# One transformer layer on one core: the last SiLUs through the exponential, sums and gate operands at other steps

## The chip, the cores and the metric

One core of one Trainium2 chip runs the whole kernel. The metric is the device time of one execution, in microseconds (us), as the median of several runs. The engines are PE (TensorE, matrix products), ACT (ScalarE), DVE (VectorE), POOL (GpSimd) and SP (SyncE, here the queue that issues nearly all transfers). Each engine executes its own instructions strictly in the order in which they stand.

## The reference

One layer over 2048 tokens of width 1024 (the rotary turning, the gates' running maxima and the norms' details are left out):

```
xn   = rms_norm(h) ; proj = xn @ w_in
q, k = split(silu(dwconv3(proj[q, k columns])))        # 1024 channels, width 3
y_a  = sigmoid(o) * rms_norm(mlstm_fwd(q, k, v) + mlstm_bwd(q, k, v))   # chunks of 128
y_b  = softmax((qn @ kn.T + qr @ kr.T) * scale) @ v     # 4 heads
h   += concat(y_a, y_b) @ w_out
u    = dwconv3(rms_norm(h) @ w_up) ; h += (silu(gate) * val) @ w_down
gate = sigmoid(rms_norm(h) @ w_ple_gate)
h   += gate * rms_norm(p @ w_ple_proj)
out  = rms_norm(h)
```

All inputs and outputs are float32. SiLU of x is x * sigmoid(x), which equals x / (1 + exp(-x)).

## The kernel before, in words

**Products.** A float32 operand is split into a high and a low half that PE can take at full rate (`split`, lines 116 to 124: ACT casts the high half, DVE subtracts to get the low one; `split_g` does it with a gain), and a product is three matrix products of halves. The large products (`w_out`, `w_up`, `w_down`, `w_ple_gate`) go in blocks by a scheme of seven products for a 2x2 block matrix; its operands B11, T1, T2, B21, T3, T4, B22 are four blocks of the weight and four sums of blocks, which were worked out before by `sum4` (line 1184) and stored.

**Order.** The stages are: `in_proj` (to about 521 us), attention with the mLSTM worked in between, the output product, the up product, the down product, and the gate with the end. Python generators are advanced in fixed places of the program text: `tail` (line 454) is what `in_proj` leaves over for the attention loop, one step at each `pump` of `attend`; `other` are the mLSTM's steps. A scheduler then sets the order on each engine from the program's order and its dependencies. Buffers go by tags: a tile of a tag waits for the last reader of the tile before it.

**The tail.** `in_proj` works through eight groups of 128 channels (j = 0 to 7) in four quarters of the tokens (c). `taps(j, c)` makes the three taps of the convolution on a 128x512 tile `ct` (one ACT, two DVE instructions); `silu(j, c, t)` applies SiLU on ACT and stores the tile to `qk_d`, from which the mLSTM loads. For j = 7 the quarters c = 2, 1, 0 are left to `tail`. Softmax of the attention needs the exponential on ACT (L934, `pe<-bk,nm`, four in each tile); its negated maximum `nm` comes from four maxima `mx<-bk` on DVE (L916), its output is transposed by PE (`tb`), split into `pt` (ACT cast and DVE L123) and multiplied (`ppv`). The mLSTM's state products are `mb<-v,kk` (L764) and its state update `cb` (L768).

**`Out.beside`** (line 1698) is called at seven places `at` of each pair of token blocks of the output product (pairs i = -8 to -1). Among other things it advances `sums(0)`: four times (k = 0 to 3) a load of four blocks of a weight with its norm's factor (`tsum`), in the next step five DVE instructions (L1196 to L1203) and four stores to `t_d`.

**`Gate.beside`** (line 1923) does the same for the gate's pairs q, from q = -9 on, alongside the down product. `proj` makes the 32 products of p with `w_ple_proj` (`fs<-pw,ph`, six matrix products each, for 16 token blocks st and two halves f); their weights lie in the places x13 and x5, the gain `gpost` in x3. `load_op` (line 1268) splits the operands of one name, `op_begin` starts a block's list of operand loads (`opr`), `op_fill` keeps up to four of them loaded ahead. For the gate (blk 6) `op_begin` was called behind the seventh place of q = -2 by the loop of `stream`. In the pair q = -1 the weights of the first gate pair are made: PE transposes of the hidden tiles (`fs<-ident,ha`), a copy to `gwr`, a split to `fw<-gwr`, and from `gwr` sums of it for the block scheme.

Of the kernel before, what the change touches and what calls it, by code (L numbers as in the profile page):

```python
# [11 lines left out]
F32R = mybir.dt.float32r  # L12
BF16 = mybir.dt.bfloat16
AF = mybir.ActivationFunctionType
ALU = mybir.AluOpType
# [4 lines left out]
P = 128  # L20
# [15 lines left out]
SB = 512  # L36
# [6 lines left out]
def pause(n):  # L43

    for _ in range(n):
        yield
# [6 lines left out]
def _rot(kind, idx):  # L53
    idx = list(idx)
    i = 0
    while True:
        yield f"{kind}{idx[i % len(idx)]}"
        i += 1


class Block:
# [114 lines left out]
    def in_proj(self):  # L176
        nc, d = self.nc, self.d
# [146 lines left out]
        for st in range(NT):  # L324
# [3 lines left out]
            t = self.at(next(trot), [P, 512], name="vo")  # L328
# [7 lines left out]
        for st in range(NT):  # L336
            ps = nat(st, ws, 512)
            t = self.at(next(trot), [P, 512], name="vo")
# [62 lines left out]
        def conv(j, c):  # L401
            silu(j, c, taps(j, c))

        def taps(j, c):
            t = self.at(next(trot), [P, 512], name="ct")
            uu, o = us[j, c // 2], (c % 2) * 512
            nc.scalar.activation(t, uu[:, o:o + 512], AF.Identity, bias=cwt[:, 3, j:j + 1], scale=cwt[:, 0, j:j + 1])
            for tap in (1, 2):
                nc.vector.scalar_tensor_tensor(t, uu[:, o + tap:o + tap + 512], cwt[:, tap, j:j + 1], t,
                                               op0=ALU.mult, op1=ALU.add)  # L410
            return t

        def silu(j, c, t):
            nc.scalar.activation(t, t, AF.Silu)
            nc.sync.dma_start(self.qk_d[4 * c:4 * c + 4, :, j, :].rearrange("c p t -> p c t"),
                              t.rearrange("p (c t) -> p c t", t=P))

# [36 lines left out]
        def tail(other):  # L454

            for i in range(2):
                self.split_kv(vals, (2 + i,))
                yield
            yield from itertools.islice(other, 7)
            ts = []  # L460
            for c in (2, 1, 0):
                ts.append(taps(7, c))
                yield
            yield from pause(3)
            for c, t in zip((2, 1, 0), ts):
                silu(7, c, t)
            yield from pause(2)
            yield from other

        return tail  # L470
# [616 lines left out]
    def split_ops(self, names):  # L1087

        items = [(n, k) for n in names for k in range(4)]
        raws = []  # L1090
        for j in range(-4, len(items)):
            if j + 4 < len(items):
                n, k = items[j + 4]
                raws.append(self.at(next(self.orot), [P, SB], name="opr"))
                self.nc.sync.dma_start(raws[-1], self.op_source(0, n, k))
            if j < 0:
                continue
            if j == 0:
                yield
            n, k = items[j]  # L1100
            if k == 0:
                self.xop[n] = self.op_places(0, n)
            self.split(raws[j], *self.xop[n][k])
            yield

# [112 lines left out]
        kt = k + i // 2 * 4  # L1218
        return self.d["w_ple_gate"][0, kt * P:(kt + 1) * P, i % 2 * SB:i % 2 * SB + SB]

    def op_places(self, blk, n):

        kk = self.BLOCKS[blk][2]
        out = []
        self.units = getattr(self, "units", {})
        for k in range(kk):
            x = self.OPX3[n][k] if kk == 3 else (self.OPXG if blk == 6 else self.OPX)[n][k // 2]
            key = blk, x
            if key not in self.units:
                self.units[key] = [self.at(f"x{x}", [P, 2, 2, SB], F32R, "op"), 0]  # L1230
            t, e = self.units[key]
            self.units[key][1] += 1
            out.append((t[:, e, 0], t[:, e, 1]))
        return out

    def op_source(self, blk, n, k):
        i = int(n[1]) - 1 if n[0] == "T" else 2 * (int(n[1]) - 1) + int(n[2]) - 1
# [10 lines left out]
    def op_begin(self, blk):  # L1248

        self.items = [(blk, n, k) for n in ("B11", "T1", "T2", "B21", "T3", "T4", "B22") for k in range(self.BLOCKS[blk][2])]  # L1250
        self.loaded, self.tag = [], None
        self.op_fill()

    def op_fill(self):

        while self.items and len(self.loaded) < 4:
            blk, n, k = self.items[0]
            if not k and (blk, n) in self.RAWS and self.tag is None:
                self.orot = _rot("t", self.RAWS[blk, n])
            self.tag = self.tag or next(self.orot)  # L1260
            if self.tag in [t for *_, t in self.loaded]:
                return
            raw = self.at(self.tag, [P, SB], name="opr")
            self.nc.sync.dma_start(raw, self.op_source(blk, n, k))
            self.loaded.append((self.items.pop(0), raw, self.tag))
            self.tag = None

    def load_op(self, blk, n):

        ops = self.xop[n] = self.op_places(blk, n)  # L1270
        for k, (hi, lo) in enumerate(ops):
            item, raw, _ = self.loaded.pop(0)
            assert item == (blk, n, k)
            gain = {1: self.g2, 2: self.g2, 6: self.g3}.get(blk)
            if gain is not None and n[0] == "B":
                kt = k + (int(n[1]) - 1) * 4
                self.split_g(raw, gain[0][:, kt:kt + 1], hi, lo)
            else:
                self.split(raw, hi, lo)
            self.op_fill()  # L1280

    def up_load(self, i):

# [116 lines left out]
    def stream(self, out):  # L1400

        nc = self.nc
# [3 lines left out]
        NUP, blocks = self.NUP, self.BLOCKS  # L1406
# [90 lines left out]
        prev, n = None, blocks[-1][0] + blocks[-1][1]  # L1497
# [7 lines left out]
        NG = NUP + 24  # L1505
        for i in range(blocks[0][0], n):
            blk = max(q for q, bl in enumerate(blocks) if bl[0] <= i)
            j = i - blocks[blk][0]
# [102 lines left out]
                    next(steps[i])  # L1611
            load(then, "T3")
            side(7)
            if any(bl[0] + bl[1] - 2 == i for bl in blocks[:-1]):
                self.op_begin(blk + 1)
            prev = s

# [20 lines left out]
class Out:  # L1638
# [59 lines left out]
    def beside(self, s, at, bank):  # L1698
        b, i = self.b, s.i
        if i > 1:  # L1700
            return

        c = 2 * i + 15 if at == 5 else 2 * i + 14
        if at in (5, 7) and 0 <= c < NT:
            self.scaled(c)
        c, f = {7: (2 * i + 15, 0), 1: (2 * i + 13, 1), 2: (2 * i + 12, 0), 3: (2 * i + 12, 1)}.get(at, (-1, 0))
        if 0 <= c < NT:
            self.turn(c, f, bank)
        if (i, at) == (-8, 1):
            self.load(-7)  # L1710
        if i < 0 and at == 5:
            self.load_x(i, 1)
            (self.load if i < -2 else b.up_load)(i + 2)
        if i < -1 and at == 6:
            self.load_x(i + 1, 0)
        if i < 0 and at == 7:
            self.tiles = self.next
        if (i, at) == (-7, 7):
            b.load_taps()
        if (i, at) == (-5, 4):  # L1720
            b.ffn_taps(bank)
        if (i, at) == (-3, 4):
            self.sums = b.sums(0)
        if (i, at) in ((-3, 4), (-3, 6), (-3, 7), (-2, 1), (-2, 2), (-2, 3), (-2, 4), (-2, 6)):
            next(self.sums)


class Gate:
# [194 lines left out]
    def beside(self, s, at, bank):  # L1923

        b, i = self.b, s.i
        q = i - self.first
        if (q, at) == (-9, 3):
            self.load_weights()
        if (q, at) == (-8, 7):
            self.split_weights()  # L1930
        if (q, at) == (-7, 2):
            self.gpost = b.row_bcast(b.at("x3", [P, D], name="gpf"), self.d["ple_post_g"][0], D)
            self.ph[0] = self.prep_p(0)
        if -7 <= q < -1 and at < 7:
            n = (q + 7) * 6 + at - 5
            if 0 <= n < 2 * NT:
                self.proj(*divmod(n, 2), bank)
        if q == -2 and at == 7:
            self.load_tile(0)
            self.load_tile(1)  # L1940

        if -1 <= q < 7 and at in (1, 2, 4, 5):
            e, f = divmod(at - 1 if at < 3 else at - 2, 2)
            self.turn(i + 1, e, f, bank)
            if f and q + e > -1 and 2 * q + e + 4 < NT:
                self.load_tile(2 * q + e + 4)
        if q == 1 and at == 1:
            self.gfin = [b.row_bcast(b.at(f"t{f}", [P, SB], name="gfin"), self.d["final_g"][f * SB:f * SB + SB], SB)
                         for f in range(2)]
        if q == -1 and at == 7:  # L1950
            self.load_tile(2)
            self.load_pj()
            self.load_pj()
        if q >= 0 and at in (2, 4):
            s.h.append(self.load_h(2 * q + at // 2 - 1))
        if q == 1 and at == 1:
            self.gfin = [b.row_bcast(b.at(f"t{f}", [P, SB], name="gfin"), self.d["final_g"][f * SB:f * SB + SB], SB)
                         for f in range(2)]
# [48 lines left out]
```

## Time and profile before

| | |
|---|---|
| runs of the kernel | 2918.75, 2919.41, 2920.72 us; median 2919.41 |
| profiled execution | 2923.7 us |
| its span on the core | 2921.9 us |
| mean granted clock of TensorE | 0.996 |
| busy: PE, DVE, ACT, POOL | 98%, 70%, 52%, 5% |

Starts in the rows are microseconds from the span's start. A bracket at a row's end is idle time of the engine ahead of the instruction, and what ended it. TensorE's granted clock (PEclk) is 1.00 at its upper level, 2.4 GHz, and half of that at its lower one; a window's value is the mean over it.

### The profile page before, as it was taken

To read this page: it belongs to the slowest core of one execution; us is meant where nothing else is said; L and a number is where in the kernel's file an instruction comes from. 1 tells how busy PE (TensorE), PEld (TensorE's weight loads), DVE (VectorE), ACT (ScalarE), POOL (GpSimd) and SP (SyncE) were. 2 spreads that over 40 slices of the span, in tenths; PEclk is the share of its full clock that TensorE was granted. 3 is DMA by queue.
4 is the path that set the end of the run, shared out by engine and by line. 5 is a ranking of instruction groups with operands and counts; after the bars stand their busy time and mean duration, and the time that the engine had idled before them with its cause. 6 is when DMAs were issued, how large, how long until landed. Compare 5 with 4: busy or idle time off the path is not lost.

```text
span 2921.9 us, 41161 instructions
## 1 busy us (share of the span) xinstructions
PE 2866.5 (98%) x14654; PEld 2424.6 (83%) x14654; DVE 2035.5 (70%) x3765; ACT 1528.3 (52%) x2984; POOL 155.1 (5%) x295
## 2 busy tenths in 40 slices
PE   8999999999999999999899999999999999999998
PEld 7888888888888889888688888888888788888787
DVE  7521555777777777766677887867777867576777
ACT  7311544656666666755655555755555423254655
POOL 3100000000000010001100000000000000001111
PEclk9999999999999999999999999999999999999999
DMA  6612545653333333467955553757776757486764
GB/s 186 132 58 80 156 117 168 205 162 114 112 108 103 96 106 113 129 215 245 307 177 173 176 190 135 230 163 229 238 238 206 247 170 266 158 265 205 268 215 162
DMA packets 406014, 513.20 MB, mean 176 GB/s; under 512 B 33824, under 2 KB 267312, under 8 KB 405808
## 3 DMA queue, kind: packets, MB, share of 16 engines
q1 hardware_dynamic: 405808, 510.57, 55.1%
q8 instruction: 115, 1.88, 0.3%
q14 instruction: 91, 0.75, 0.1%
HBM read 328.35 MB, written 182.12 MB: 175 GB/s over the span
## 4 chain that ended last, share of the span: by engine, by line
PE 83%; DMA 6%; DVE 5%; ACT 3%; issue 2%; POOL 1%; SPq 0%; ACTq 0%; POOLq 0%; DVEq 0%
PE fy L1419 19%; PE fz L1419 13%; PE bk L133 13%; PE fx L1419 13%; PE ppv L133 5%; PE tb L974 3%; PE bk L911 2%; PE bk L915 2%; PE bk L913 2%; PE bk L912 2%; PE bk L914 2%; PE fs L133 1%; PE gb L133 1%; PE mb L849 1%; DMA h_d<-xt 1%
## 5 line engine op out<-in xcount | busy, mean ns | idle before, releaser
L1419 PE MATMUL fz<-op,fw 128*128 128x512 f32 x1968 | 479.2, 391 | 8.1 <-ACT fw L120 4.9
L1419 PE MATMUL fx<-op,fw 128*128 128x512 f32 x1968 | 479.6, 391 | 0.9 <-ACT op L128 0.7
L1419 PE MATMUL fy<-op,fw 128*128 128x512 f32 x1968 | 475.6, 390 | 1.7 <-ACT ug L1561 1.5
L1419 PEld LDWEIGHTS fz<-op,fw 128*128 128x128 f32 x1968 | 368.3, 188 | 85.7 <-ACT fw L120 6.1
L1419 PEld LDWEIGHTS fy<-op,fw 128*128 128x128 f32 x1968 | 368.7, 188 | 79.4 <-ACT ug L1561 1.9
L1419 PEld LDWEIGHTS fx<-op,fw 128*128 128x128 f32 x1968 | 369.0, 188 | 78.1 <-ACT op L128 1.9
L1419 PE MATMUL fy<-op,fwd 128*128 128x512 f32 (+1 forms) x984 | 238.0, 390 | 3.3 <-DVE uv L1404 1.7
L120 ACT CAST pt<-tb 128x512 fp32r<-128x512 f32 x256 | 147.2, 586 | 167.9 <-PE tb L974 167.2
L133 PE MATMUL bk<-wsp,xh 128*128 128x512 f32 (+1 forms) x768 | 234.4, 386 | 0.0
L916 DVE TENSOR_REDUCE mx<-bk 128x1 f32<-128x512 f32 x256 | 175.0, 685 | 64.4 <-PE bk L915 60.2
L1419 PEld LDWEIGHTS fy<-op,fwd 128*128 128x128 f32 x984 | 182.7, 188 | 42.1 <-DVE uv L1404 2.8
L133 PE MATMUL ppv<-pt,kv 128*128 128x256 f32 x1536 | 206.5, 288 | 1.8 <-ACT pt L120 1.5
L123 DVE TENSOR_TENSOR pt<-tb,pt 128x512 fp32r<-128x512 f32 x256 | 174.4, 685 | 29.8 <-ACT pt L120 27.7
L934 ACT ACTIVATE pe<-bk,nm 128x512 f32<-128x512 f32 x256 | 174.5, 694 | 35.9 <-DVE nm L928 32.4
L133 PEld LDWEIGHTS ppv<-pt,kv 128*128 128x128 f32 x1536 | 190.2, 192 | 2.5 <-ACT pt L120 1.8
L133 PEld LDWEIGHTS bk<-wsp,xh 128*128 128x128 f32 x768 | 145.4, 189 | 25.1
L133 PE MATMUL bk<-wsp,xl 128*128 128x512 f32 (+1 forms) x384 | 150.8, 393 | 8.4 <-DVE xl L123 8.4
L133 PE MATMUL bk<-xh,wqk 128*128 128x512 f32 x480 | 157.4, 393 | 0.0
L974 PE MATMUL tb<-ident,pe 128*128 128x128 f32 x1024 | 151.4, 274 | 4.8 <-DVE pt L123 4.1
L974 PEld LDWEIGHTS tb<-ident,pe 128*128 128x128 f32 x1024 | 122.0, 141 | 24.3 <-DVE pt L123 6.3
L120 ACT CAST fw<-hraw 128x1024 fp32r<-128x1024 f32 (+1 forms) x72 | 70.2, 981 | 119.0 <-PE fx L1419 61.2
L123 DVE TENSOR_TENSOR fw<-fwr,fw 128x1024 fp32r<-128x1024 f32 x88 | 107.5, 1221 | 24.1 <-ACT fw L120 24.1
(360 smaller groups left out, 4925.5 us busy)
## 6 DMA issues: line engine op xcount, KB each, us to landing
fwr<-in_w_up SPq DMA_DIRECT2D x66, 512.0 KB, 4.8
fh<-h_d SPq DMA_DIRECT2D x48, 512.0 KB, 4.6
h_d<-fh SPq DMA_DIRECT2D x48, 512.0 KB, 3.6
s_d<-fwr SPq DMA_DIRECT2D x44, 512.0 KB, 2.8
fws<-s_d SPq DMA_DIRECT2D x44, 512.0 KB, 3.7
rw<-row_d SPq DMA_DIRECT2D x32, 512.0 KB, 5.5
tw_d<-tsum SPq DMA_DIRECT2D x60, 256.0 KB, 5.4
opr<-tw_d SPq DMA_DIRECT2D x60, 256.0 KB, 4.9
```

The lines of the kernel that those rows point to most:

```text
L120: nc.scalar.copy(hi, src)
L123: (sub or nc.vector).tensor_tensor(lo, src, _f(hi), op=ALU.subtract)
L133: mm = lambda *a, **k: self.nc.tensor.matmul(*a, **k, skip_group_check=more)
L911: mm(ps, ql, kh[:, ks], start=True, stop=False)
L912: mm(ps, qr, self.krl[:, ks], start=False, stop=False)
L913: mm(ps, qh, kl[:, ks], start=False, stop=False)
L914: mm(ps, qr, self.kr2[:, ks], start=False, stop=False)
L915: mm(ps, qh, kh[:, ks], start=False, stop=True)
L916: nc.vector.tensor_reduce(s.mx[:, kb:kb + 1], ps, axis=AX.X, op=ALU.max)
L934: nc.scalar.activation(s.pe[:, kb % 2], s.banks[kb], AF.Exp, bias=s.nm, scale=ASCALE, accum_out=s.rs[:, kb:kb + 1])
L974: nc.tensor.transpose(t[:, j, :], s.p[kb][:, j * P:(j + 1) * P], self.ident)
L1419: nc.tensor.matmul(out, a[:, k * P:(k + 1) * P], parts[lo][:, cols], start=first, stop=lo == 1 and k == last, skip_group_check=more)
```

## The change

Three edits. First, the tail's three SiLUs become exp(-x) on ACT, into a tile `ce` of tag t6, and on DVE a clamp with the added one, a reciprocal and a product; each is spread over more steps of the generator. Second, the steps of `sums(0)` in `Out.beside` are taken at other places, so that two or three places lie between a load and its sums. Third, the gate's projection products are made two places sooner, and `op_begin` for the gate is called at the fifth place of q = -2; at places 6 and 7 the operands k = 2 and 3 of B11, T2 and T3 are split. `op_place` now takes one k at a time. The rest of the diff is the same code in another form.

```diff
         def silu(j, c, t):
             nc.scalar.activation(t, t, AF.Silu)
+            store_qk(j, c, t)
+
+        def store_qk(j, c, t):
             nc.sync.dma_start(self.qk_d[4 * c:4 * c + 4, :, j, :].rearrange("c p t -> p c t"),
...
             for c in (2, 1, 0):
                 ts.append(taps(7, c))
                 yield
-            yield from pause(3)
+
             for c, t in zip((2, 1, 0), ts):
-                silu(7, c, t)
-            yield from pause(2)
+                e = self.at("t6", [P, 512], name="ce")
+                nc.scalar.activation(e, t, AF.Exp, scale=-1.0)
+                yield
+                nc.vector.tensor_scalar(e, e, 1.0e38, 1.0, op0=ALU.min, op1=ALU.add)
+                nc.vector.reciprocal(e, e)
+                yield
+                nc.vector.tensor_tensor(t, t, e, op=ALU.mult)
+                store_qk(7, c, t)
             yield from other
...
     def op_begin(self, blk):
 
         self.items = [(blk, n, k) for n in ("B11", "T1", "T2", "B21", "T3", "T4", "B22") for k in range(self.BLOCKS[blk][2])]
+        self.soon, self.early = (blk == 6) * [(blk, n, k) for n in ("B11", "T2", "T3") for k in (2, 3)], {}
+        self.items = self.soon + [item for item in self.items if item not in self.soon]
         self.loaded, self.tag = [], None
         self.op_fill()
...
     def load_op(self, blk, n):
 
-        ops = self.xop[n] = self.op_places(blk, n)
-        for k, (hi, lo) in enumerate(ops):
-            item, raw, _ = self.loaded.pop(0)
-            assert item == (blk, n, k)
...
+        self.xop[n] = [self.early.get((blk, n, k)) or self.split_op() for k in range(self.BLOCKS[blk][2])]
+
+    def split_soon(self, n):
+
+        for _ in range(n):
+            item = self.loaded[0][0]
+            self.early[item] = self.split_op()
...
-            if any(bl[0] + bl[1] - 2 == i for bl in blocks[:-1]):
+            if i < NG - 2 and any(bl[0] + bl[1] - 2 == i for bl in blocks[:-1]):
                 self.op_begin(blk + 1)
...
-        if (i, at) in ((-3, 4), (-3, 6), (-3, 7), (-2, 1), (-2, 2), (-2, 3), (-2, 4), (-2, 6)):
+        for _ in range({(-3, 4): 1, (-3, 7): 2, (-2, 2): 2, (-2, 5): 2, (-2, 7): 1}.get((i, at), 0)):
             next(self.sums)
...
-        if (q, at) == (-7, 2):
+        if (q, at) == (-8, 7):
             self.gpost = b.row_bcast(b.at("x3", [P, D], name="gpf"), self.d["ple_post_g"][0], D)
             self.ph[0] = self.prep_p(0)
         if -7 <= q < -1 and at < 7:
-            n = (q + 7) * 6 + at - 5
+            n = (q + 7) * 6 + at - 3
             if 0 <= n < 2 * NT:
                 self.proj(*divmod(n, 2), bank)
+        if q == -2 and at > 4:
+            b.split_soon(3) if at > 5 else b.op_begin(6)
```

Lines of the changed kernel are 9 to 16 higher than those of the same statement before (L916 is L925, L768 is L777).

DVE, the third attention tile after the tail has begun, before (`mx` maxima of the scores, `gt` the softmax's sum, `pt` the low halves of the transposed probabilities, `nm` the negated maximum):

```order
L916 TENSOR_REDUCE mx<-bk 128x1
L939 TENSOR_REDUCE gt<-rs 128x1
L940 RECIPROCAL gt<-gt 128x1
L916 TENSOR_REDUCE mx<-bk 128x1
L123 TENSOR_TENSOR pt<-tb,pt 128x4x128
L916 TENSOR_REDUCE mx<-bk 128x1
L123 TENSOR_TENSOR pt<-tb,pt 128x4x128
L916 TENSOR_REDUCE mx<-bk 128x1
L123 TENSOR_TENSOR q_s<-q_t,q_s 128x256
L927 TENSOR_REDUCE nm<-mx 128x1
L123 TENSOR_TENSOR pt<-tb,pt 128x4x128
```

DVE, the same tile of the changed kernel, from its first maximum on (`ce` the exponential's tile, `ct` the convolution's, `cb` the mLSTM's state):

```order
L925 TENSOR_REDUCE mx<-bk 128x1
L473 RECIPROCAL ce<-ce 128x512
L766 SCALAR_TENSOR_TENSOR kk<-kk,cols 128x512
L475 TENSOR_TENSOR ct<-ct,ce 128x512
L925 TENSOR_REDUCE mx<-bk 128x1
L123 TENSOR_TENSOR pt<-tb,pt 128x4x128
L472 TENSOR_SCALAR ce<-ce 128x512
L925 TENSOR_REDUCE mx<-bk 128x1
L473 RECIPROCAL ce<-ce 128x512
L777 SCALAR_TENSOR_TENSOR cb<-cb,cols,mb 128x129
L475 TENSOR_TENSOR ct<-ct,ce 128x512
```

Each `pt` of this tile now stands behind one more reciprocal; the third reciprocal follows in the same tile, seven rows after the last one shown, between the second `pt` and the third.

ACT, the pair q = -1, around the second weight cast of the gate, before (`op` casts of gate operands, `gwr` the turned hidden tiles, `fw` the weights' high halves):

```order
L1807 COPY gwr<-fs 128x512 x2
L120 CAST op<-opr 128x512
L120 CAST fwd<-gwr 128x512
L120 CAST op<-opr 128x512
L128 ACTIVATE op<-opr,gt 128x512 x3
L1796 ACTIVATE junk,nt_s<-fh 128x1024
L128 ACTIVATE op<-opr,gt 128x512
L120 CAST fw_25238<-gwr 128x1024
L1531 COPY fy<-fx 128x512
```

ACT, the same place of the changed kernel:

```order
L1823 COPY gwr<-fs 128x512 x2
L128 ACTIVATE op<-opr,gt 128x512
L120 CAST fwd<-gwr 128x512
L128 ACTIVATE op<-opr,gt 128x512 x3
L1812 ACTIVATE junk,nt_s<-fh 128x1024
L120 CAST fw_25259<-gwr 128x1024
L120 CAST op<-opr 128x512
L1547 COPY fy<-fx 128x512
```

Two of six operand casts between the copies and the weight cast are gone here; counted from the copy `fy<-fx` ahead of these rows there were 15, and there are 11.

## Rows read from the trace of the kernel before

**Rows 1.** The profile page: busy us (share), instructions by engine; the chain that ended last.

```profile
PE 2866.5 (98%) x14654; PEld 2424.6 (83%) x14654; DVE 2035.5 (70%) x3765; ACT 1528.3 (52%) x2984; POOL 155.1 (5%) x295
...
PE 83%; DMA 6%; DVE 5%; ACT 3%; issue 2%; POOL 1%; SPq 0%; ACTq 0%; POOLq 0%; DVEq 0%
```

**Rows 2.** PE in order of time, 521 to 532 us: start, duration, engine, line.

```profile
521.25 0.60 PE L974 MATMUL tb<-ident,pe 128*128 128x128 f32 x4
524.01 0.91 PE L764 MATMUL mb<-v,kk 128*128 128x129 f32 x4 [2.16 <-issue]
526.28 1.23 PE L764 MATMUL mb<-v,kk 128*128 128x129 f32 x4 [1.36 <-DVE cb L768]
527.16 0.78 PE L911 MATMUL bk<-kv,q_s 128*128 128x512 f32 x1
...
531.15 0.40 PE L915 MATMUL bk<-kv,q_s 128*128 128x512 f32 x1
```

**Rows 3.** ACT in order of time, 522 to 526 us.

```profile
522.60 1.28 ACT L414 ACT_TABLE_LOAD   x1
523.89 0.63 ACT L414 ACTIVATE ct<-ct 128x512 f32<-128x512 f32 x1
524.54 1.28 ACT L934 ACT_TABLE_LOAD   x1
525.84 0.69 ACT L934 ACTIVATE pe<-bk,nm 128x512 f32<-128x512 f32 x1
```

**Rows 4.** PE in order of time around one attention tile, 560 to 571 us.

```profile
560.98 0.39 PE L912 MATMUL bk<-kr,q_t 128*128 128x512 f32 x1
561.21 0.39 PE L913 MATMUL bk<-kv,q_s 128*128 128x512 f32 x1
...
567.48 3.11 PE L133 MATMUL ppv<-pt,kv 128*128 128x256 f32 x24
```

**Rows 5.** PE in order of time after 1420 us.

```profile
1420.46 2.56 PE L1419 MATMUL fz<-op,fw 128*128 128x512 f32 x10 [3.13 <-ACT op L120]
```

**Rows 6.** Line 673 alone: ns min/median/max, first and last start, form.

```profile
L673 DVE RECIPROCAL gtmp<-gtmp x1: 954/954/954, 139.5 to 139.5; 128x128 f32<-128x128 f32 x1
```

**Rows 7.** Groups of DVE instructions by line and form: busy us, mean ns.

```profile
L916 DVE TENSOR_REDUCE mx<-bk 128x1 f32<-128x512 f32 x256 | 175.0, 685 | 64.4 <-PE bk L915 60.2 <-DMA qk_d<-ct 3.3
...
L940 DVE RECIPROCAL gt<-gt 128x1 f32<-128x1 f32 x64 | 10.4, 162 | 1.6
```

**Rows 8.** Line 1200 alone, the same columns as rows 6.

```profile
L1200 DVE TENSOR_SCALAR tsum<-tsum,gt x12: 480/482/490, 1361.5 to 2215.1; 128x512 f32<-128x512 f32 x12
```

**Rows 9.** Window 530 to 540: length, busy us by engine, PEclk, DMA share.

```profile
530.00:540.00 10.00, 10.00 (x68) 8.93 (x67) 8.28 (x19) 6.85 (x10) 0.00 (x0) 0.94 0.69 200
```

**Rows 10.** PE in order of time at 1391 us.

```profile
1391.89 1.12 PE L1694 MATMUL fs<-ident,xt 128*128 128x128 f32 x4 [4.03 <-ACT xt L1685]
```

**Rows 11.** DVE in order of time, 1388 to 1390 us.

```profile
1388.91 0.48 DVE L1200 TENSOR_SCALAR tsum<-tsum,gt 128x512 f32<-128x512 f32 x1
1389.30 0.68 DVE L1404 TENSOR_TENSOR xt<-xt,fz 128x512 f32<-128x512 f32 x1
```

**Rows 12.** PE in order of time on both sides of 2739 us.

```profile
2736.32 2.89 PE L1419 MATMUL fx<-op,fw 128*128 128x512 f32 x12
2742.70 1.85 PE L1419 MATMUL fz<-op,fw 128*128 128x512 f32 x4 [3.49 <-ACT fw L120]
```

**Rows 13.** ACT in order of time, 2733 to 2743 us.

```profile
2733.18 1.14 ACT L120 CAST op<-opr 128x512 fp32r<-128x512 f32 x2 [0.52 <-DMA opr<-tw_d]
...
2735.79 0.62 ACT L120 CAST op<-opr 128x512 fp32r<-128x512 f32 x1 [0.49 <-DMA opr<-tw_d]
...
2738.69 1.37 ACT L128 ACTIVATE op<-opr,gt 128x512 fp32r<-128x512 f32 x2 [0.31 <-DMA opr<-in_w_ple_gate]
...
2741.62 1.03 ACT L120 CAST fw<-gwr 128x1024 fp32r<-128x1024 f32 x1
```

**Rows 14.** Window 2740 to 2750, the same columns as rows 9.

```profile
2740.00:2750.00 10.00, 7.30 (x26) 5.83 (x27) 9.87 (x15) 6.26 (x11) 1.80 (x2) 0.83 0.90 294
```

More of the change, by code (lines that the diff above doesn't have):

```diff
@@ L1101, in split_ops @@
             if k == 0:
-                self.xop[n] = self.op_places(0, n)
+                self.xop[n] = []
+            self.xop[n].append(self.op_place(0, n, k))
             self.split(raws[j], *self.xop[n][k])
@@ L1219, in w_gate, with op_place @@
         return self.d["w_ple_gate"][0, kt * P:(kt + 1) * P, i % 2 * SB:i % 2 * SB + SB]
-    def op_places(self, blk, n):
-        kk = self.BLOCKS[blk][2]
-        out = []
+    def op_place(self, blk, n, k):
+        x = self.OPX3[n][k] if self.BLOCKS[blk][2] == 3 else (self.OPXG if blk == 6 else self.OPX)[n][k // 2]
         self.units = getattr(self, "units", {})
[L1226 to L1234, printed above, removed]
+        if (blk, x) not in self.units:
+            self.units[blk, x] = [self.at(f"x{x}", [P, 2, 2, SB], F32R, "op"), 0]
+        unit = self.units[blk, x]
+        unit[1] += 1
+        return [unit[0][:, unit[1] - 1, e] for e in range(2)]
     def op_source(self, blk, n, k):
@@ L1257, in op_fill @@
             blk, n, k = self.items[0]
-            if not k and (blk, n) in self.RAWS and self.tag is None:
+            if (not k or self.items[0] in self.soon[:1]) and (blk, n) in self.RAWS and self.tag is None:
                 self.orot = _rot("t", self.RAWS[blk, n])
@@ L1268, in load_op, with split_op @@
     def load_op(self, blk, n):
-        ops = self.xop[n] = self.op_places(blk, n)
-        for k, (hi, lo) in enumerate(ops):
-            item, raw, _ = self.loaded.pop(0)
-            assert item == (blk, n, k)
[L1274 to L1280, printed above, removed]
+        self.xop[n] = [self.early.get((blk, n, k)) or self.split_op() for k in range(self.BLOCKS[blk][2])]
[3 more added lines that the diff above has]
+            self.early[item] = self.split_op()
+    def split_op(self):
+        (blk, n, k), raw, _ = self.loaded.pop(0)
+        hi, lo = self.op_place(blk, n, k)
+        gain = {1: self.g2, 2: self.g2, 6: self.g3}.get(blk)
+        if gain is not None and n[0] == "B":
+            kt = k + (int(n[1]) - 1) * 4
+            self.split_g(raw, gain[0][:, kt:kt + 1], hi, lo)
+        else:
+            self.split(raw, hi, lo)
+        self.op_fill()
+        return hi, lo
     def up_load(self, i):
```

## The prediction

> **What bounds the kernel.** I read the page first: TensorE (PE) is busy for 2866.5 us and holds 83% of the chain that ended last [rows 1]. Matrix work alone fills nearly all of the span of 2921.9 us, so an edit is worth only what it does to PE's idle time and to PE's clock; a microsecond saved on ACT or DVE counts where PE waits for just that. Then I read the chain of waits on PE and went to the three places that the change touches, in order of time.
>
> *The seam between projection and attention (521 to 531 us).* PE ends its transposes at 521.85, starts again at 524.01 and waits once more, 1.36 us, before 526.28 [rows 2]. What it is short of is the next exponentials of the softmax, which empty the score banks. ACT could have begun them at 522.60; it loads a table instead, runs a SiLU, loads the first table again, and reaches the exponential at 525.84 [rows 3]. The waits drop the granted clock to its lower level: from 527.16 to 531.15 nine steps take 3.99 us, 0.44 each, where 0.23 is the step at the upper level [rows 2, 4].
>
> *The sums at 1391 us.* PE waits 4.03 us for a scaled tile [rows 10] whose last residual add stands on DVE behind a step of the sums [rows 11].
>
> *The gate's first products (2739 us).* PE has run its fx products by 2739.2 and waits 3.49 us for a weight cast of ACT, `fw<-gwr`, that starts at 2741.62 [rows 12, 13]. The window after it has a granted clock of 0.83 [rows 14].
>
> **The change, part by part.** The sums are made against the profiled execution: 2923.7 us, span 2921.9.
>
> *A, first half: what the table loads cost.* The built order of the changed kernel has no table load in these tiles: exp(-x) stands among the softmax's exponentials. What goes at the seam: the waits of 2.16 and 1.36, together 3.52; in the nine steps 3.99 - 9 x 0.23 = 1.92 of clock; and half of the two state groups that ran at the lower level, 0.91 and 0.88 (526.28 to 527.16), so 0.9. Sum 6.3 us. What stays: the first exponential can start at 522.60 and takes 0.69, so PE stands from 521.85 to 523.3, 1.45 us. Does that cost clock? A wait of 3.13 us elsewhere was followed by ten products in 2.56 us, still at the upper level [rows 5], so I take no. First half: -6.3 + 1.45 = **-4.9 us** (-3.2 if the clock falls here after all and costs what rows 14 show, 1.7).
>
> *A, second half: what the exponential's way costs.* Three SiLUs of 0.63 leave ACT and three exponentials of about 0.69 come, which is nothing, since the loads made room. DVE gets three groups of tensor_scalar, reciprocal and multiply on 128x512. The tensor_scalar is 0.48 [rows 8], the multiply like another full pass, 0.69 [rows 7]. No 128x512 reciprocal ran before. The nearest rows: 954 ns for 128x128 [rows 6] and 162 ns for 128x1 [rows 7]. Slope: (954 - 162) / 127 = 6.24 ns a column; for 512 columns 162 + 511 x 6.24 = **3.35 us** each. Lower end: a plain pass, 0.69 us. Upper end: four 128x128 ones, 3.8 us. I take 3.35, since both rows are the same instruction.
>
> Engines run their queues in order, so what counts is what stands behind the reciprocals. In the third tile of the changed order all three stand in one tile, each ahead of a `pt` subtraction (the low half of a transposed probability) which the `ppv` products need. Walk from that tile's first score product, T = 0, with full passes 0.6 apart (they overlap by about 0.09, as 1388.91 + 0.48 against 1389.30 shows [rows 11]), score groups of 5 x 0.23, twelve `ppv` products at 3.11/24 each (1.5) [rows 4], transposes 0.35:
> - The first exponential is done at about 1.3, tensor_scalar 1.85, a maximum 2.45, reciprocal to 5.8, then `kk`, multiply, maximum, `pt`: 8.2. PE has done four score groups and two transposes by 5.3: wait **2.9**.
> - PE then has 2.1 of work (12 `ppv`, state products, transposes), to 10.3. DVE: tensor_scalar, maximum, reciprocal to 12.7, `cb`, multiply, `cb`, `pt` at 14.5: wait **4.2**. The next exponential shares one buffer with the last multiply (tag t6) and is ready in time.
> - PE to 16.7; DVE by the same row reaches the third `pt` at 20.9: wait **4.2**.
>
> Sum 11.3 us. Against it stands room: DVE is busy 8.28 of 10 us here [rows 9], and the `wos` sums that ran here move to later rows. That is why DVE keeps no backlog after this tile; inside it nothing can pass a reciprocal. Clock: the wait of 3.49 cost 0.17 x 10 = 1.7 us in its window [rows 14], the one of 3.13 nothing [rows 5]. Two waits here are over 4 us; the slow stretch behind the first of them lies in the shadow of the next wait, so I charge it once, 1.7. Second half: **+13.0 us** (from +3.3 with reciprocals of 0.69: each us off a reciprocal takes some 3 us off the three waits).
>
> A rule of the Trainium skill speaks for a dearer reciprocal: *VectorE: DVE Perf Modes*, First, the fixed hardware budget, says that the reciprocal is an iterative divide with a repeat count of 8. Eight passes at the slope of the maximum, (685 - 162)/511 = 1.02 ns, would be an estimate of 4.3 us each, and the total below would be +5.5 instead of +2.6. The 128x128 row, 954 ns, is nearer to six passes than to eight, and I go by the row.
>
> A: -4.9 + 13.0 = **+8.1 us**.
>
> *B, the sums.* The steps are the same, with more time between load and sum. On DVE one tensor_scalar of 0.48 goes from ahead of the residual add to behind it [rows 11], so the wait of 4.03 may shrink by that: **-0.5 us**. On SP's queue one store to `x_d` now goes ahead of four `t_d` stores; a tile late there would cost about one transfer issue behind it. Bounds -1 to +1.5; that the longer distance frees PE of nothing more is likely, since PE waits there for an add and not for a load.
>
> *C, the gate.* PE's products are the same ones, the projection's six each two steps earlier. Of the operand casts between the copy `fy<-fx` ahead of it and the weight cast, 15 stood on ACT; 11 do now. Four of some 0.62 us [rows 13] are 2.5 us, and the waits for operand transfers in between, 0.52 + 0.49 + 0.31 = 1.3 us [rows 13], should go since those transfers are issued earlier. The cast would then end at 2742.65 - 3.8 = 2738.9, before PE asks at 2739.2. Gain: 3.49 and the clock's 1.7, less a rest of 0.2: **-5.0 us**. If the transfers are as late as before, a wait of 1.0 stays and the clock is kept: -4.2. If the early casts wait for their own transfers and hold the queue, the bound is 0. What is queued behind them on ACT in the step before is the projection's squares and two casts of the down products' inputs, which PE multiplies only one step later; that hides it. DVE loses the four low halves too, in a stretch where it is busy 9.87 of 10 [rows 14].
>
> **Sum:** +8.1 - 0.5 - 5.0 = +2.6, so 2926.3 us for the execution profiled. That execution is 4.3 above the median of the runs, 2919.41; against the median the forecast is **2922.0 us**. A difference under 0.2% (5.8 us, so 2913.6 to 2925.2) can hardly be told from no change here.
>
> **Rivals.**
> 1. *The reciprocals cost what a plain pass costs, and the change is faster.* Place: the third tile. At 0.69 us the three waits shrink from 11.3 to about 3.3, without loss of clock; A becomes -4.9 + 3.3 = -1.6, the total -7.1: 2912.3. It decides below some 1.1 us per reciprocal. For it: DVE has 1.7 us free in 10 [rows 9]. Against: the 954 ns row [rows 6].
> 2. *The tile is dearer.* Reciprocals of 3.8 us (+1.4) and the lower clock charged at two more places, the seam and behind the second wait (+3.4): total +7.4, 2926.8. For it: clock losses came after both long waits that I read [rows 2, 14]; against: the wait of 3.13 that cost none [rows 5]. The eight passes of *VectorE: DVE Perf Modes* in the Trainium skill belong to this rival, and are in its chance.
> 3. *The gate's stall only changes its name.* PE waits for the next late operand instead of the cast, since ACT waits for transfers and the DMA share is 0.90 [rows 14]. C becomes 0, total +7.6, 2927.0. For it: ACT's own waits name transfers [rows 13]; against: four casts really leave that stretch.
> 4. *B does not do what it says:* the sums wait as before. The total is +3.1, inside the first case.
>
> **Numbers.** Forecast 0.53 (2917 to 2925.5, its own range), rival 1 0.16, rival 2 0.19, rival 3 0.12. The range that leaves 2 in 10 out reaches from rival 1 to somewhat beyond rival 3: 2911 to 2929. Faster than 2913.6: most of rival 1 and a little of the forecast's lower edge, 0.15; slower than 2925.2: most of rivals 2 and 3 and the forecast's upper edge, 0.32; the same 0.53.
>
> **What would show it.** In the profile after: no table load between 522 and 540 us; a reciprocal of about 3.3 us for 128x512, three times; PE waits of some 3, 4 and 4 us named after `pt` in one attention tile near 540 us, and a granted clock under 1 there; the 4.03 us wait at 1391 a little shorter; no wait over 1 us at `fz<-op,fw` near 2740 and a granted clock of 1.0 there. I am wrong if the reciprocal is under 1.5 us, if PE finds other work while `pt` is late, or if the gate's stall stays.

## The result, and the profile after

| | before | changed |
|---|---|---|
| median (15 runs each, same chip) | 2919.35 us | 2926.16 us |
| lowest to highest | 2916.25 to 2924.76 | 2923.97 to 2931.06 |
| ratio | | 1.0024 [1.0016, 1.0032] |
| span of the profiled execution | 2921.9 us | 2927.2 us |

The change makes the kernel slower by 7 us: 0.24%, a little over the 0.2% under which the prediction would not tell a difference from no change. The forecast was 2922.0, in a range of 2911 to 2929; the narrower range of the forecast's own case, 2917 to 2925.5, does not hold the result. Two of the executions profiled in the experiments ran at a mean granted clock of 0.654 and are not read; their kernels were run again.

**The third attention tile.** DVE in order of time after (start, duration, engine, line, operation); they give the duration that [rows 6] could only bound:

```profile
545.57 3.34 DVE L473 RECIPROCAL ce<-ce 128x512 f32<-128x512 f32 x1
...
550.57 0.68 DVE L123 TENSOR_TENSOR pt<-tb,pt 128x512 fp32r<-128x512 f32 x1
...
552.10 3.34 DVE L473 RECIPROCAL ce<-ce 128x512 f32<-128x512 f32 x1
...
556.46 0.68 DVE L123 TENSOR_TENSOR pt<-tb,pt 128x512 fp32r<-128x512 f32 x1
...
558.05 3.34 DVE L473 RECIPROCAL ce<-ce 128x512 f32<-128x512 f32 x1
...
562.40 0.68 DVE L123 TENSOR_TENSOR pt<-tb,pt 128x512 fp32r<-128x512 f32 x1
```

And PE in the same stretch:

```profile
521.87 0.50 PE L920 MATMUL bk<-kv,q_s 128*128 128x512 f32 x1 [1.78 <-ACT pe L943]
...
523.78 0.63 PE L922 MATMUL bk<-kv,q_s 128*128 128x512 f32 x1
...
543.72 0.40 PE L921 MATMUL bk<-kr,q_t 128*128 128x512 f32 x1
...
551.30 0.65 PE L983 MATMUL tb<-ident,pe 128*128 128x128 f32 x4 [1.06 <-DVE pt L123]
...
556.52 0.71 PE L773 MATMUL mb<-v,kk 128*128 128x129 f32 x4 [3.14 <-DVE cb L777]
...
562.47 0.66 PE L761 MATMUL mb<-ident,kTb 128*128 128x128 f32 x4 [1.72 <-DVE cb L777]
...
564.82 0.40 PE L921 MATMUL bk<-kr,q_t 128*128 128x512 f32 x1
```

Three `pt` come about 6 us apart, each behind one reciprocal of 3.34 us, and PE stops three times. From the second score product of this tile (543.72) to that of the next one (564.82) 21.1 us pass; the same pair before is 10.1 us apart:

```profile
549.25 0.39 PE L912 MATMUL bk<-kr,q_t 128*128 128x512 f32 x1
...
559.36 0.39 PE L912 MATMUL bk<-kr,q_t 128*128 128x512 f32 x1
```

Two windows of the changed kernel's execution, columns as in [rows 9], show the clock: 0.83 behind the wait of 1.78 us (a product takes 0.63 at 523.78 where it takes 0.39 otherwise) and 0.87 in the tile with the reciprocals.

```profile
520.00:530.00 10.00, 8.21 (x38) 6.70 (x38) 7.72 (x17) 5.06 (x13) 0.00 (x0) 0.83 0.41 123
...
550.00:560.00 10.00, 5.75 (x37) 5.20 (x36) 10.00 (x15) 2.43 (x4) 0.00 (x0) 0.87 0.35 105
```

**The seam.** PE's wait of 1.78 us at 521.87 is for an exponential. The two waits before, 2.16 and 1.36 us in [rows 2], were not; DVE in the trace of before:

```profile
523.23 0.68 DVE L757 SCALAR_TENSOR_TENSOR kk<-kk,cols 128x512 f32<-128x512 f32 x1
...
525.88 0.34 DVE L768 SCALAR_TENSOR_TENSOR cb<-cb,cols,mb 128x129 f32<-128x129 f32 x1
```

The product at 524.01 starts 0.1 us behind the end of `kk`, which it multiplies, and the one at 526.28 starts 0.06 us behind the end of `cb`. Both belong to the mLSTM, and both stand on PE ahead of the score products. In the changed kernel the mLSTM's next state products come only at 538.38 and 540.29, and the score products stand first.

**The sums.** The wait that [rows 10] shows is 1.76 us shorter:

```profile
1397.18 1.11 PE L1710 MATMUL fs<-ident,xt 128*128 128x128 f32 x4 [2.27 <-ACT xt L1701]
```

**The gate.** PE after, where [rows 12] stood before, and a wait that is new, for a hidden tile `ha`:

```profile
2727.89 0.63 PE L1822 MATMUL fs<-ident,ha 128*128 128x128 f32 x4 [0.22 <-DMA ha<-h_d]
...
2747.62 1.20 PE L1435 MATMUL fz<-op,fw 128*128 128x512 f32 x4 [2.65 <-ACT fw L120]
```

ACT ahead of that wait, to be held against [rows 13]:

```profile
2733.11 0.62 ACT L120 CAST op<-opr 128x512 fp32r<-128x512 f32 x1 [1.52 <-DMA opr<-tw_d]
...
2737.25 0.62 ACT L120 CAST op<-opr 128x512 fp32r<-128x512 f32 x1 [1.95 <-DMA opr<-tw_d]
2737.77 1.05 ACT L1812 ACTIVATE junk<-fh 128x1024 bf16<-128x1024 f32 x1
...
2738.83 2.17 ACT L120 CAST op<-opr 128x512 fp32r<-128x512 f32 x4
...
2744.84 0.72 ACT L128 ACTIVATE op<-opr,gt 128x512 fp32r<-128x512 f32 x1 [0.51 <-DMA opr<-in_w_ple_gate]
...
2746.52 1.04 ACT L120 CAST fw<-gwr 128x1024 fp32r<-128x1024 f32 x1
```

SP's queue shows why ACT waits at 2737.25: the four operand loads stand behind a load `fh`, which goes out only at 2730.66. Ahead of its first row stands the row of DVE whose end, at 2723.75, lets the load `ha` go.

```profile
2722.80 0.95 DVE L123 TENSOR_TENSOR fw<-hraw,fw 128x768 fp32r<-128x768 f32 x1
...
2723.78 0.32 SPq L1806 DMA_DIRECT2D ha<-h_d  x1
...
2730.66 0.32 SPq L1346 DMA_DIRECT2D fh<-h_d  x1
2731.08 1.81 SPq L1271 DMA_DIRECT2D opr<-tw_d  x4
```

The stall at the weight cast fell from 3.49 to 2.65 us, no more, and the clock fell behind it too (0.94 and 0.89 in the windows from 2740 and 2750 us). That is this one execution: the same edit leaves less of the stall in runs 2, 3, 11 and 12 (the table behind run 10).

### The profile page after: what moved, and what is told of

It is laid out like the page before. It is cut to its first block, busy times and chain, and to the rows that moved or that the text cites. A ratio compares the mean times of both kernels' runs of the same rounds, so it can differ in the third digit from the quotient of the medians.

```text
span 2927.2 us, 41168 instructions
## 1 busy us (share of the span) xinstructions
PE 2868.5 (98%) x14654; PEld 2425.6 (83%) x14654; DVE 2047.7 (70%) x3774; ACT 1524.7 (52%) x2980; POOL 158.4 (5%) x295
## 3 DMA queue, kind: packets, MB, share of 16 engines
q8 instruction: 115, 1.88, 0.3%
## 4 chain that ended last, share of the span: by engine, by line
PE 51%; DMA 4%; DVE 2%; ACT 1%; issue 1%; SPq 0%; POOL 0%; POOLq 0%; ACTq 0%; DVEq 0%
PE fy L1435 20%; PE fz L1435 14%; PE fx L1435 13%; PE fs L133 1%; DMA opr<-tw_d 1%; PE ppv L133 1%; DMA opr<-t_d 1%; DVE op L123 1%; DMA t_d<-tsum 1%; DMA tsum<-x_d 0%; DMA opr<-in_w_down 0%; ACT op L120 0%; PE fs L1822 0%; PE tb L983 0%; DMA fwr<-in_w_up 0%
## 5 line engine op out<-in xcount | busy, mean ns | idle before, releaser
L925 DVE TENSOR_REDUCE mx<-bk 128x1 f32<-128x512 f32 x256 | 175.0, 685 | 54.5 <-PE bk L924 50.5
```

The source lines that it names most:

```text
L925: nc.vector.tensor_reduce(s.mx[:, kb:kb + 1], ps, axis=AX.X, op=ALU.max)
```

## The experiments

Ratios are to runs of the kernel before on the same chip, with a 95% interval. One per mille is 2.9 us.

**1. The exponential's way alone** (the kernel before with the first edit of the diff and no other).

> The kernel before with the exponential's way for the last three SiLUs alone. Theory (the loss is all in the tail): 8 to 11 us slower than before, about 2929, with three reciprocals of 3.34 us and the waits of 1.06, 3.14 and 1.72 us again. Rival (the two other edits do the harm, or the start of the execution differs by chance): within 3 us of before.

Measured: 2931.22 us, ratio 1.0034 [1.0021, 1.0046], so +9.9 us. The reciprocals are 3.34 us again, and PE's waits in the third tile 1.06, 3.13 and 1.85 us. All of the loss is here.

**2. Sums and gate without the exponential's way** (the second and third edit).

> The change without the exponential's way: sums and gate edits alone. Theory: 2 to 3 us faster than before, about 2916.5 to 2917.5 (1.9 from the sums, 0.5 from the gate). Rival (the gate edit brought its 5 us and something else ate it in the whole change): 6 to 7 us faster.

Measured: 2919.70 us, 0.9991 [0.9982, 0.9999]: -2.6 us. With run 1 the parts add to +7.3, and the whole change measured +7.0.

**3. The gate edit alone.**

> The gate edit alone. Theory: the stall at the second weight cast keeps 2.6 us and the clock still falls; 0 to 1 us faster than before. Rival: with the attention in its old order the operand transfers come in time and it is 4 to 5 us faster.

Measured: 2918.16 us, 0.9992 [0.9984, 1.0001]: -2.3 us, between the two expectations. PE in this run:

```profile
2721.94 0.63 PE L1813 MATMUL fs<-ident,ha 128*128 128x128 f32 x4 [0.80 <-DMA ha<-h_d]
...
2740.40 1.19 PE L1426 MATMUL fz<-op,fw 128*128 128x512 f32 x4 [1.38 <-ACT fw L120]
```

The old stall is down to 1.38 us without a fall of the clock; but PE now also waits for hidden tiles, 0.80 us here and 0.61 us at 2747.07. The stall was partly renamed.

**4. The sums alone.**

> The sums edit alone. Theory: the wait of 4.03 us near 1391 becomes about 2.3; 1.5 to 2 us faster. Rival (the shorter wait in the whole change came from the other alignment of the queues): no more than 0.5 us faster.

Measured: 2919.77 us, 0.9998 [0.9989, 1.0007]: -0.6 us, with both signs in the interval. The wait near 1391 is 2.63 us. Over all runs it is 4.03, 3.96, 3.31, 2.93, 3.04, 4.22 and 3.17 with the old sums (before, runs 1, 3, 5, 6, 9 and 10) and 2.27, 2.27, 2.63, 1.68 and 1.88 with the new ones (the whole change, runs 2, 4, 11 and 12): shorter by 1.4 us in the mean. That the wait is shorter is shown; what it gives in time is below what these runs can tell.

**5. The exponential's way with almost no reciprocal.**

```diff
-                nc.vector.reciprocal(e, e)
+                nc.vector.reciprocal(e[:, 0:1], e[:, 0:1])
```

> The exponential's way alone, but the reciprocal is taken of one column of the 512, so the three tiles are not divided (left out: 511 of 512 columns of the division). Theory (the reciprocals ahead of the pt subtractions are the loss): the loss of 9.9 us goes, and what is left is the gain of the table loads, 2 to 4 us faster than before; no wait over 1.5 us in that tile. Rival (the other order of the mLSTM's steps is the loss): still 5 us slower or more.

Measured: 2918.15 us, 0.9996 [0.9987, 1.0005]. The loss of run 1 is gone: from 1.0034 to 0.9996 is 11 us, uncertain by 4 to 5 us with both intervals, for three reciprocals of 3.34. The third tile, from second score product to second score product, as above:

```profile
541.54 0.39 PE L921 MATMUL bk<-kr,q_t 128*128 128x512 f32 x1
...
553.32 0.40 PE L921 MATMUL bk<-kr,q_t 128*128 128x512 f32 x1
```

11.8 us where the changed kernel takes 21.1. But the gain that both my theory and my prediction counted on beside it, 2 to 5 us for the table loads, is only -1.2 us, and nothing is an equally good reading. The list of PE's waits from 515 to 1245 us says where a part of it went (us in total, times, longest):

```profile
PE bk L920 <- ACT pe L943: 3.2, 3, 1.8
PE mb L887 <- DVE hy L882: 3.1, 3, 1.5
```

Two of these waits late in the attention:

```profile
1195.03 0.50 PE L887 MATMUL mb<-ident,hy 128*128 128x128 f32 x2 [1.47 <-DVE hy L882]
...
1211.55 0.50 PE L920 MATMUL bk<-kv,q_s 128*128 128x512 f32 x1 [1.14 <-ACT pe L943]
```

The seam's wait is 1.78 us in place of 2.16 and 1.36. But the waits for the exponentials and for the mLSTM's output `hy` were 1.1 and 1.6 us in total before; less the seam's own 1.78 they have grown by 1.8 us. Adding up all idle time of PE from 515 us to the attention's last `ppv` product gives 14.9 us before and 16.0 us here: the seam got shorter, and the attention did not. (It is 13.3 to 15.7 us in runs 2, 3, 4, 10 and 12, whose attention is the old one, and 13.8 in run 6.)

**6. SiLU by tanh, which needs no division.** SiLU is x * (0.5 + 0.5 tanh(x/2)).

```diff
-                nc.scalar.activation(e, t, AF.Exp, scale=-1.0)
+                nc.scalar.activation(e, t, AF.Tanh, scale=0.5)
                 yield
-                nc.vector.tensor_scalar(e, e, 1.0e38, 1.0, op0=ALU.min, op1=ALU.add)
-                nc.vector.reciprocal(e, e)
+                nc.vector.tensor_scalar(e, e, 0.5, 0.5, op0=ALU.mult, op1=ALU.add)
```

> SiLU as x times (0.5 + 0.5 tanh(x/2)), which needs no reciprocal and, as the built order shows, no table load beside the exponentials; everything else as in the exponential's way alone. Theory: like the run with one column, 2 to 4 us faster than before. Rival: 5 us slower or more.

Measured: 2918.57 us, 1.0002 [0.9993, 1.0011]. Neither expectation holds to the letter: the loss is gone, as in run 5, and so is the gain. No table load stands between the tanh instructions and the exponentials in the trace. The Trainium skill says why in *ScalarE: Activation LUTs*, Table sets: the hidden batching unit: tanh is in the exponential's set. The trace agrees: none of its three tanh has a load ahead of it. They take 0.63 to 0.65 us each, like the SiLUs.

**7 and 11. The whole change with tanh**, the diff of run 6 on top of the changed kernel.

> The whole change with tanh in place of exponential and reciprocal. Theory: the sum of the parts, 2 to 4 from the tail and 2.6 from sums and gate: 4 to 7 us faster than before. Rival (parts do not add): no faster than sums and gate alone, 2.6.

Measured: 2915.36 us, 0.9987 [0.9978, 0.9996].

> The whole change with tanh, timed again and with a profile. Theory: 3 to 5 us faster than before; idle time of PE in the attention about as before, since what the missing table loads give at the seam is given back by later waits of the mLSTM. Rival: the seam's gain stays, 6 us faster or more.

Measured: 2914.82 us, 0.9986 [0.9978, 0.9995]: 4 us faster than before and 11 us faster than the changed kernel. Idle time of PE in the attention, added up in the same way, is 15.3 us here and 15.7 us in run 12, whose attention is that of the kernel before. The traces also say when the seam's gain goes. The table has the time from the attention's first score product to the last `ppv` product of a tile, lowest to highest and mean; at each of these ends PE has done the same number of products in all nine traces.

| end of tile | old attention (before, runs 2, 3, 4, 10, 12) | new order without reciprocals (runs 5, 6, 11) | mean difference |
|---|---|---|---|
| 6 | 93.4 to 95.4, 94.4 us | 88.9 to 89.9, 89.6 us | 4.8 |
| 16 | 205.1 to 207.3, 206.3 | 201.6 to 203.3, 202.4 | 3.9 |
| 46 | 552.9 to 555.1, 554.1 | 550.1 to 551.8, 550.9 | 3.2 |
| 58 | 691.9 to 694.0, 693.0 | 690.7 to 692.5, 691.7 | 1.3 |
| 64, the last | 745.3 to 747.8, 746.5 | 745.6 to 747.3, 746.4 | 0.1 |

The gain is there and lasts through two thirds of the attention; most of it goes in the last third, where the new order has its longest waits behind the seam for `hy` and for an exponential.

PE's gate waits in run 11:

```profile
2715.25 0.63 PE L1821 MATMUL fs<-ident,ha 128*128 128x128 f32 x4 [1.66 <-DMA ha<-h_d]
2733.00 1.21 PE L1434 MATMUL fz<-op,fw 128*128 128x512 f32 x4 [0.70 <-ACT fw L120]
```

**8 and 10. The projection two places earlier, without early operands** (of the third edit only the two lines on `gpost` and on n).

> Of the gate edit only the projection's two earlier places, no early operands. Theory (the early operand casts stand ahead of the last two casts of the down products' inputs, and these hold the buffers of the hidden tiles): no PE wait for the hidden tiles, and the wait at the second weight cast about as long as before, 3 to 4 us; time within 1 us of before. Rival (the projection's move makes the hidden tiles late): waits of 0.5 to 1.6 us for the hidden tiles here too.

Measured: 2917.99 us, 0.9996 [0.9987, 1.0005].

> The projection's two earlier places alone, looked at again. Theory: hidden tiles in time, no PE wait for them over 0.3 us; the wait at the second weight cast between 2 and 3.5 us, as 14 of 15 operand casts still stand before it. Rival: waits of 0.5 us or more for the hidden tiles.

Measured, one run of 2920.6 us. PE has no wait for the hidden tiles, as the theory said; the wait at the weight cast is 1.58 us, which is less than it said:

```profile
2737.31 1.20 PE L1419 MATMUL fz<-op,fw 128*128 128x512 f32 x4 [1.58 <-ACT fw L120]
2738.80 3.41 PE L1419 MATMUL fz<-op,fw 128*128 128x512 f32 x8 [0.28 <-DVE fw L123]
```

So part of what shortens the stall is the projection's own move, and no wait for the hidden tiles is seen without the early operands. The load of the first hidden tile goes out late in run 10 too, though. SP and PE before, and then in run 10:

```profile
2714.74 0.32 SPq L1790 DMA_DIRECT2D ha<-h_d  x1
...
2721.62 0.60 PE L1806 MATMUL fs<-ident,ha 128*128 128x128 f32 x4
```

```profile
2714.63 0.32 SPq L1790 DMA_DIRECT2D ha<-h_d  x1
...
2718.70 0.60 PE L1806 MATMUL fs<-ident,ha 128*128 128x128 f32 x4
```

Before, the load is issued 6.9 us ahead of its use; in run 10 4.1 us, and in the traces with early operands 3.9 us ahead of the moment when PE asks. All traces side by side, for the weight cast and the hidden tiles up to 30 us behind the first of them:

| traces | wait at the weight cast, us | lower clock at it | waits for `ha`, us |
|---|---|---|---|
| before, runs 1, 4, 5, 6, 9 (old gate) | 3.49, 4.12, 3.63, 3.64, 3.62, 3.54 | in all six | none |
| run 10 (projection alone) | 1.58 | yes | none |
| runs 2, 3, 11, 12 (gate edit) | 0.79, 1.38, 0.70, 1.67 | in none | 2.10, 1.41, 1.66, 1.58 |
| the whole change | 2.65 | yes | 0.22 |

Both waits together are 3.5 to 4.1 us with the old gate and 2.4 to 3.3 us with the edit, which is 0.8 us less in the mean. The rest of the 2.3 us that run 3 gained would be the fall of the clock, which four of the five traces with the edit do not have; the prediction read 1.7 us for it from [rows 14]. This split is an estimate.

**9. Each reciprocal twice.**

```diff
                 nc.vector.reciprocal(e, e)
+                nc.vector.reciprocal(e, e)
```

> The exponential's way alone with each reciprocal made twice, so the tiles are multiplied by 1 + exp(-x) where they were divided. Theory (every microsecond of reciprocal ahead of a pt subtraction is a microsecond of PE): three more times 3.34, so 10 us slower than the exponential's way alone, about 20 us slower than before. Rival (most of the second reciprocal lies beside PE's work): 3 us or less on top.

Measured: 2938.28 us, 1.0066 [1.0051, 1.0081]: +19.3 us against +9.9 with one each. PE in the third tile:

```profile
541.82 0.40 PE L922 MATMUL bk<-kr,q_t 128*128 128x512 f32 x1
...
552.59 1.11 PE L984 MATMUL tb<-ident,pe 128*128 128x128 f32 x4 [4.26 <-DVE pt L123]
...
561.18 1.09 PE L984 MATMUL tb<-ident,pe 128*128 128x128 f32 x4 [2.74 <-DVE pt L123]
...
570.37 1.65 PE L133 MATMUL ppv<-pt,kv 128*128 128x256 f32 x6 [3.22 <-DVE pt L123]
...
572.52 0.63 PE L922 MATMUL bk<-kr,q_t 128*128 128x512 f32 x1
```

The tile takes 30.7 us: 11.8, 21.1 and 30.7 with none, one and two of them, 9.3 and 9.6 us for 10.0 us of reciprocals. That settles the mechanism: a reciprocal on DVE ahead of `pt` goes to PE at nearly its full length, in waits and in products at the lower clock.

**12. Sums and gate once more**, beside the version with tanh.

> Sums and gate edits alone, timed beside the version with tanh on one chip. Theory: 2 to 3 us faster than before and within 2 us of the version with tanh. Rival: that version is 3 us faster than this one.

Measured: 2916.53 us, 0.9991 [0.9982, 1.0000]. The version with tanh is 0.5 per mille below it, which the intervals do not separate.

## Why the prediction was right in its range, and where its terms were off

- *Reciprocals (+13.0).* The price of one, 3.35 us, measured 3.34. The eight passes that *VectorE: DVE Perf Modes* (First, the fixed hardware budget) in the Trainium skill led to would have been 4.3 us by the estimate made there. The trace is at 6.2 ns a column, as the slope from the 128x128 row said. What the reciprocals cost the kernel is 11 us (run 1 against run 5) or 9 us (against run 6), and 9.4 for a second set (run 9), each uncertain by 4 to 6 us. The step was right; the walk was dear by some 2 to 4 us. It let PE run out of products 5.3 us into the tile, where the trace has them until 6.8 us in, and let the waits grow to 2.9, 4.2 and 4.2 us where the trace has 1.06, 3.14 and 1.72 and a part of the rest as products at the lower clock. Two of the three waits are named after `cb` and not, as forecast, after `pt`; they end with the `cb` update that stands behind the reciprocal and just ahead of `pt`.
- *Table loads (-4.9).* This is the step that failed, in its reading and in its size. I read the waits of 2.16 and 1.36 us as PE short of the next exponentials. The rows of the seam above show that they ended with `kk` and `cb` on DVE, and the exponential of 525.84 was done at 526.53, before PE came to the score products at 527.16. The wait at the seam did shrink, from 3.52 to 1.78 us (I had 1.45), but with another order of PE's products; that the missing loads by themselves bring it is not shown. But runs 5 and 6, which have no table load and no reciprocal, are not measurably faster than before, -1.2 and +0.6 us. I took the seam's local gain as a gain of the stage. The gain was 4.8 us at the end of the sixth tile and 0.1 us at the end of the attention; PE lost the time again in small waits, late in the attention above all, for `hy` and for an exponential. Removing the table loads bought nothing that lasted.
- *What I called nothing or hidden.* The lower clock after the seam's wait: in the changed kernel it fell, in runs 1, 5, 6, 9 and 11 it did not, after the same wait. The forecast's "no" held in five of these six traces.
- *Sums (-0.5).* The direction was right; the wait shrank by 1.4 us in the mean, nearly three times what I gave it. The time of run 4 alone does not confirm a gain of that size.
- *Gate (-5.0).* Mis-sized by half: -2.3 us in run 3, and the wait of 2.65 us in the whole change is one that the prediction said would not be there. Two things failed. First, "that hides it", said of what the early casts hold up. The load of the first hidden tile waits in all traces for the end of a low half of the down products' inputs on DVE, which ACT's cast precedes. In the changed kernel it is issued 3.9 us ahead of the moment when PE asks for the tile, before 6.9 us ahead. Of these 3.0 us the projection's move accounts for 2.8, as run 10 shows: between the load's issue and the first hidden tile PE ran 30 products before, six of them the projection's, and 17 in run 10. The early casts add 0.2 us. In run 10 the tile was there in time all the same; with the early operands it came 4.1 to 5.6 us behind the load's issue, and PE waited 0.2 to 1.7 us. Two operand loads go out ahead of it then, in the 2.5 us before. That they slow it is likely, not shown. Second, I counted on the operand transfers in q = -1 to come sooner, and on ACT's waits for them to go. They wait on SP behind the load of `fh`, and ACT waits 1.52, 1.95 and 0.51 us where [rows 13] have 0.52, 0.49 and 0.31; after 2737.25 it has all the casts that are left to do in a row. This is rival 3, at half its price.
- *The sum.* Forecast +2.6, measured +7.0: about +10 of tail where I had +8.1, and -2.6 of sums and gate where I had -5.5. Both misses have the same root, a wait removed locally that came back under another name. The result lies beyond the forecast's own range (up to 2925.5) and next to the sums of rivals 2 and 3 (2926.8 and 2927.0), though the reciprocals were not dearer, as rival 2 had it. That it came no further out is partly luck: the reciprocals were forecast 2 to 4 us too dear, which made up for half or so of what the table loads (about 4 to 5 us) and the gate (2.7 us) were forecast too favourably.

What stays open: why the rest of the attention gives the seam's gain back. The runs show where it goes, and that the new order has larger waits there, but no run here holds that order fixed while it takes the table loads away.

## What to carry to other kernels

Before an activation is rewritten to save a table load, look for a function in the table that is already loaded which needs no division: tanh did what exponential and reciprocal did, without 10 us of DVE in front of the matmul's operands. Price a new instruction by what stands behind it in its engine's queue; here that made a microsecond on a DVE that was busy 70% of the time cost a microsecond of the whole. And when products and casts are moved earlier, ask not only who reads their results, but also which load used the time that they took: here the load of the first hidden tile went out 6.9 us ahead of its use before and 3.9 us after. A wait that is gone is a gain of the stage only if the stage ends earlier; compare two traces at points where the same number of products is done.

## What the runs showed of the hardware

A wait of nearly one length did not always have the same effect on the clock. After the seam's 1.78 us the granted clock fell in the changed kernel (the window from 520 to 530 us has 0.83, above); in run 5, after the same 1.78 us at the same place, it stayed at the upper level:

```profile
520.00:530.00 10.00, 8.72 (x55) 7.65 (x56) 8.99 (x19) 5.97 (x16) 0.00 (x0) 1.00 0.41 131
```

In the prediction I had charged the clock by the length of a wait, with 3.13 us as one that costs nothing and 3.49 as one that costs 1.7 us. That is too simple: 2.27 us at 1397 in the changed kernel was followed by a granted clock of 0.86 in the window from 1390 and 1.38 us in run 3 by none under 1. At the gate's weight cast 1.58 us in run 10 was followed by 0.87 in the window from 2740, and 1.67 us in run 12 by 1.00 in the windows on both sides of it:

```profile
2734.80 1.19 PE L1426 MATMUL fz<-op,fw 128*128 128x512 f32 x4 [1.67 <-ACT fw L120]
```

A fall behind one wait can differ between executions and should be given a chance, not a threshold.
